# A PSUM bank for the samples' softmax, prompt attention in a lane of its own, and parted gathers

## The chip, the cores and the metric

The kernel runs on one core of a Trainium2 chip, in one launch. The metric is device time in microseconds (us). Three runs of the kernel before took 1416.22, 1419.79 and 1420.54 us; their median, 1419.79 us, is the time to compare with. What can be told from no change is about 0.3% of it, some 4.3 us.

## The reference, cut to what matters

One inference step of one layer on 512 prompt tokens and on 8 samples, each of which has 4096 past positions in a paged cache.

```python
conv_in, a, b, z, qa, kva = split_in(rmsnorm(h, g_attn) @ w_in)          # one combined projection
q, k, v, g, beta = gdn_prep(causal_conv(ext, w_conv), a, b, ...)         # group A
o_gdn = gdn_output(gdn_chunked(q, k, v, g, beta), z, g_gdn_out)          #   prompt: delta rule in chunks of 64
o_mla = mla_prompt_attention(q_nope, q_rope, k_nope, k_rope, v)          # group B, prompt: causal softmax, 8 heads
# group B, samples: for every page of the cache
kn_p, v_p = mla_expand(ckv_pool[pages], w_kv_b, g_k_nope)                #   keys are expanded to be normed
sc_p = (qn . kn_p + qr . kr_pool[pages]) * SCALE;  online softmax;  acc += p @ v_p
h = h + concat(o_gdn, o_mla) @ w_o;  h = h + ffn(rmsnorm(h));  h + (p @ w_ple_proj) * sigmoid(...)
```

Everything is float32; a weight product is made of three products of a high and a low part.

## The kernel before, in words

The spine of the program is the loop over the samples' keys at the end of `kern`: 8 samples of 32 key tiles of 128 positions. For a tile, TensorE transposes the gathered latents (`ps_cT`, L1387), ScalarE and VectorE split them (`cth`, `ctl`), and 12 matmuls of 260 columns (`ps_K`, L1453) give the expanded keys, with the sample's four scores of each half as extra columns. ScalarE squares the keys (`sqk`), VectorE sums them (`ssq`), and every 8 tiles GpSimd makes their norms (`key_norms`).

When the 32 tiles of a sample are done, `softmax_pv` works as a generator: a maximum over all keys with two small matmuls (`ps_m`), the exponential `pw`, then 33 matmuls of the weights with the gathered latents (`ps_pv`, L1358), then the sums (`ps_l`). It advances by a step per key tile of the next sample. The gathered latents of a sample stay in their buffers until `ps_pv` has read them. These buffers (`raw`, four tiles each, eight per sample) are a ring of `NR0 + NR1 = 11`; `gathers` also fetches the rotary keys (`kr`, ring of `NKR = 10`) in the same breath. `rotary` multiplies them with the rotary queries.

All else that does not depend on the samples is a filler: `mixers` is one generator through latent heads, projection (`project_qkv`, `convolve`, `gate`), then `delta_rule` and `prompt_heads` side by side (weights 0.6 and 0.4), then `split_mixers`. Per key tile it advances by `PACE = 1.45` steps. Heads of the prompt's attention therefore come only when the projection is over.

PSUM has eight banks: four for `ps_mm` (two buffers of two), one for `ps_c` (the transposed latents), one for `ps_s`, one each for `ps_f0` and `ps_f1`. `pss` hands out `ps_s`: to the softmax of the samples (`ps_m`, `ps_pv`, `ps_l`), to `rotary`, and in `prompt_heads` to the transposed keys and to the transposed probabilities `ps_pT` (L785). `psf(0)` carries one half of the projection, the convolution's transposes, the prompt's queries, scores (`ps_sc`) and output (`ps_o`, L796); `psf(1)` the other half and all of `delta_rule`. A bank that is asked for anew waits until its last reader is done.

The order in which each engine runs is fixed when the program is built: a scheduler with a timeline estimate places the instructions of the loop, which the program gives it in the order told above, and every engine then works through its own list in order. So an instruction that waits holds up all that stands behind it on its engine.

In `delta_rule`, per-row factors go to DRAM (`fac_d`, 48 rows of 512, L1013) and come back spread over partitions: `db` (L1037) for each of four tiles, 24 pieces of 64 floats for every partition, and `bk` (L1123) for the scaling on GpSimd at L1124.

After the loop come the output projection (`ps_wog`, `ps_wom`), the feed-forward and the gate, in one stretch of matmuls that the change does not touch.

Of the kernel before, what the change touches and what calls it, by code (L numbers as in the profile page):

```python
# [16 lines left out]
P = 128  # L17
# [11 lines left out]
PACE = (1.45, 1.45, 1.45)  # L29
# [40 lines left out]
def kern(tc, I, O, dbg=None, stop=99):  # L70
# [137 lines left out]
    NR0, NR1, NKR = 4, 7, 10  # L208
# [472 lines left out]
    def project_qkv(tiles):
# [3 lines left out]
        for i in tiles:  # L685
            w = load_win(i)
            ct = cv.tile([P, NT], F32, tag="ct", name=f"ct{i}")
            for hf in range(2):
                ps = psf(hf, f"ps_in{i}{hf}")
# [12 lines left out]
            conv = convolve(i, ct, psf(0, f"ps_n{i}")) if i < 12 else gate(i, ct)  # L702
# [3 lines left out]
    def gate(i, ct):  # L706
        th = cv.tile([P, NT], F32, tag="th", name=f"thz{i}")
# [36 lines left out]
    def prompt_heads():  # L744
        mh = mhp[0]
        for h in range(8):
            vv = mh.tile([P, 4, P], F32R, tag="vv", name=f"vv{h}")
            nc.sync.dma_start(f(vv), v_d[:, :, h].rearrange("p t a c -> p t (a c)"))
            parts = []
            for src, lab in ((q_d, "q"), (k_d, "k")):  # L750
                nat = mh.tile([P, 4, 96], F32, tag=lab + "n", name=f"{lab}n{h}", bufs=1)
                nc.sync.dma_start(nat, src[:, :, h, :])
                pk = psf(0, f"ps_{lab}T{h}") if lab == "q" else pss(f"ps_{lab}T{h}")
# [9 lines left out]

            off = (0, 512, 896, 1152)
            pth = mh.tile([P, 1280], F32R, tag="pth", name=f"pth{h}", bufs=1)
            ptl = mh.tile([P, 1280], F32R, tag="ptl", name=f"ptl{h}", bufs=1)
            for i in range(4):
# [208 lines left out]
    def delta_rule():  # L976
# [149 lines left out]
        for _ in range(3):  # L1126
            yield
# [558 lines left out]
```

## Time and profile before

| | us |
|---|---|
| median of three runs | 1419.79 |
| the profiled execution, its own time | 1427.76 |
| its span, first to last instruction | 1426.0 |
| TensorE matmuls busy in the span | 1349.3 (95%) |
| VectorE, ScalarE, GpSimd busy | 815.9, 586.8, 640.0 |
| mean granted clock of TensorE | 0.958 |

The loop over the keys begins near 97 us; the last key tile and the output projection lie before 945 us, and from there to the end at 1426 us there is nothing but the tail. In the profile the granted clock is 1.0 at 2.4 GHz and 0.5 at 1.2 GHz, so a stretch with 0.90 spent a fifth of its time at the lower level. The busy time of TensorE counts what runs at the lower level in full; to see what a stretch lost, one needs both its idle time and its clock.

### The profile page before, as it was taken

How to read it: one execution, taken by the hardware profiler on the slowest of the kernel's cores; microseconds unless marked ns; L12 is line 12 of the kernel's file. 1: busy time of each engine (PE TensorE's matmuls, PEld its weight loads, DVE VectorE, ACT ScalarE, POOL GpSimd, SP SyncE). 2: the span in 40 equal slices, each digit the busy share in tenths (PEclk: the TensorE clock that was granted, in tenths of full speed). 3: DMA queues.
4: the chain of work that ended last, by engine and by line, in shares of the span. 5: the costliest groups of instructions: out<-in, count | busy, mean ns of one | idle time of the engine just before them, and what ended most of it. 6: DMA issues, size and time to landing. Idle time of an engine off the chain costs nothing.

```text
span 1426.0 us, 27926 instructions
## 1 busy us (share of the span) xinstructions
PE 1349.3 (95%) x11094; PEld 1273.6 (89%) x11094; DVE 815.9 (57%) x1659; ACT 586.8 (41%) x1342; POOL 640.0 (45%) x809
## 2 busy tenths in 40 slices
PE   4889988999999898999999998999999999999998
PEld 2789977999988796997897896999999999999998
DVE  3747784655669575565683674546666566411164
ACT  3336543543455464644452464433222222222232
POOL 5222645453354497435342333546444444454531
PEclk8899998999999999999996898999999999999999
DMA  7322215234233415304323403243333333233231
GB/s 262 104 104 82 88 56 176 55 70 127 83 86 66 160 31 161 87 27 132 52 43 95 125 13 106 76 132 90 89 89 90 94 99 90 85 90 95 88 111 39
DMA packets 198806, 133.61 MB, mean 94 GB/s; under 512 B 65272, under 2 KB 183315, under 8 KB 198668
## 3 DMA queue, kind: packets, MB, share of 16 engines
q1 hardware_dynamic: 187412, 94.06, 24.2%
q0 software_dynamic: 11264, 37.76, 7.9%
q8 instruction: 88, 1.44, 0.4%
q14 instruction: 42, 0.34, 0.1%
HBM read 117.89 MB, written 14.00 MB: 92 GB/s over the span
## 4 chain that ended last, share of the span: by engine, by line
PE 80%; DVE 8%; DMA 4%; issue 4%; ACT 2%; POOL 1%; SPq 1%; another core or an unknown queue 1%; DVEq 0%; ACTq 0%; POOLq 0%
PE ps_K L1453 21%; PE ps_d L1588 9%; PE ps_u L1270 9%; PE ps_g L1270 9%; PE ps_in L693 7%; PE ps_pg L1270 3%; PE ps_cT L1387 3%; PE ps_pv L1358 2%; PE ps_wom L1549 1%; PE ps_wog L1300 1%; PE ps_natB L375 1%; DVE ssq L1458 1%; PE ps_natA L375 1%; PE ps_pp L1621 1%; PE ps_kr L1319 1%
## 5 line engine op out<-in xcount | busy, mean ns | idle before, releaser
L1453 PE MATMUL ps_K<-wkh,cth 128*128 128x260 f32 x1024 | 226.8, 301 | 10.7 <-ACT S L1457 6.4
L1458 DVE TENSOR_REDUCE ssq<-sqk 128x8 f32<-128x512 f32 x256 | 173.8, 681 | 85.6 <-ACT sqk L1456 80.5
L1456 ACT ACTIVATE sqk<-ps_K 128x512 f32<-128x512 f32 x256 | 152.7, 597 | 157.5 <-PE ps_K L1453 134.0
L1453 PE MATMUL ps_K<-wkl,cth 128*128 128x260 f32 x1024 | 215.9, 290 | 0.0
L1453 PE MATMUL ps_K<-wkh,ctl 128*128 128x260 f32 x1024 | 215.5, 291 | 0.0
L1453 PEld LDWEIGHTS ps_K<-wkh,cth 128*128 128x128 f32 x1024 | 165.0, 195 | 14.0 <-ACT S L1457 7.1
L1453 PEld LDWEIGHTS ps_K<-wkl,cth 128*128 128x128 f32 x1024 | 164.9, 195 | 0.1
L1453 PEld LDWEIGHTS ps_K<-wkh,ctl 128*128 128x128 f32 x1024 | 163.2, 194 | 0.6 <-issue 0.3
L1393 DVE TENSOR_TENSOR ctl<-ps_cT,cth 128x512 fp32r<-128x512 f32 x128 | 87.5, 684 | 48.3 <-ACT cth L1392 43.4
L1392 ACT ACTIVATE cth<-ps_cT 128x512 fp32r<-128x512 f32 x128 | 77.1, 602 | 46.0 <-PE ps_cT L1387 36.3
L336 POOL DMA_INDIRECT kr<-in_cache_krope_dram,idx x64 | 62.7, 979 | 69.2 <-PE ps_kr L1314 54.8
L334 POOL DMA_INDIRECT raw<-in_cache_ckv_dram,idx x64 | 61.4, 959 | 55.0 <-PE ps_pv L1358 26.3
L126 POOL TENSOR_TENSOR wg_l<-wg_r,wg_h 128x1024 fp32r<-128x1024 f32 x22 | 53.6, 2436 | 71.9 <-ACT wg_h L125 71.9
L1387 PE MATMUL ps_cT<-cst,raw 128*128 128x128 f32 x512 | 81.5, 282 | 3.0 <-DVE ctl L1393 2.1
L126 POOL TENSOR_TENSOR wu_l<-wu_r,wu_h 128x1024 fp32r<-128x1024 f32 x22 | 52.7, 2396 | 66.6 <-ACT wu_h L125 66.6
L126 POOL TENSOR_TENSOR wd_l<-wd_r,wd_h 128x1024 fp32r<-128x1024 f32 (+1 forms) x24 | 53.0, 2210 | 65.8 <-ACT wd_h L125 65.8
L693 PE MATMUL ps_in<-xh,win_h 128*128 128x260 f32 x256 | 73.6, 288 | 0.7 <-ACT win_h L125 0.7
L102 POOL TENSOR_SCALAR rs<-ssq 128x64 f32<-128x64 f32 x24 | 7.0, 290 | 148.6 <-DVE ssq L1458 130.4
L693 PE MATMUL ps_in<-xh,win_l 128*128 128x260 f32 x256 | 72.6, 285 | 0.0
L693 PE MATMUL ps_in<-xl,win_h 128*128 128x260 f32 x256 | 72.3, 283 | 0.0
L1270 PE MATMUL ps_g<-ul,wg_h 128*128 128x260 f32 x352 | 71.0, 283 | 0.9 <-DVE ul L1517 0.7
L1270 PE MATMUL ps_u<-uh,wu_l 128*128 128x260 f32 x352 | 71.7, 283 | 0.0
(597 smaller groups left out, 3638.4 us busy)
## 6 DMA issues: line engine op xcount, KB each, us to landing
wg_r<-in_w_ffn_gate_dram SPq DMA_DIRECT2D x22, 512.0 KB
wu_r<-in_w_ffn_up_dram SPq DMA_DIRECT2D x22, 512.0 KB
win_r<-in_w_in_dram SPq DMA_DIRECT2D x32, 256.0 KB
wd_r<-in_w_ffn_down_dram SPq DMA_DIRECT2D x16, 512.0 KB
wpg_r<-in_w_ple_gate_dram SPq DMA_DIRECT2D x8, 512.0 KB
db<-fac_d SPq DMA_DIRECT2D x8, 384.0 KB
wd_r<-in_w_ffn_down_dram SPq DMA_DIRECT2D x8, 384.0 KB
xres<-xT_d SPq DMA_DIRECT2D x8, 260.0 KB
```

Of the source, the lines that this page charges most:

```text
L126: gp.tensor_tensor(out=lo, in0=raw, in1=f(hi), op=ALU.subtract)
L334: gp.indirect_dma_start(out=raws[G].rearrange("p t c -> p (t c)"), out_offset=None, in_=ckv_rows, in_offset=off)
L336: gp.indirect_dma_start(out=krs[G], out_offset=None, in_=kr_rows, in_offset=off)
L693: te.matmul(ps[:, :HN], w[q][a][:, k, :], (xh, xl)[b][:, q * 4 + k, hf * HN:(hf + 1) * HN], start=q + k + a + b == 0, stop=q + k == 4 and ...
L1270: te.matmul(o[hf], w[a][:, k, :], mov[b][:, k, hf * HN:(hf + 1) * HN], start=k == 0 and (a, b) == (0, 0), stop=k == K - 1 and a == 1)
L1387: te.transpose(pt[:, (s * 2 + k) * P:(s * 2 + k + 1) * P], raw[:, (n % 2) * 2 + s, k * P:(k + 1) * P], ident)
L1392: sc.activation(hi, p4, AF.Copy)
L1393: ve.tensor_tensor(out=lo, in0=p4, in1=f(hi), op=ALU.subtract)
L1453: te.matmul(pk[:, hf, :260], x[:, s * 2 + k, :], y[:, k, hf, c0:c0 + 260], start=k == 0 and x is cur[0] and y is wkh, stop=k == 1 and x is ...
L1456: sc.activation(sq, pk[:, :, wo:wo + 256], AF.Square)
L1458: ve.tensor_reduce(out=ssq[:, i, :], in_=sq.rearrange("p f (h c) -> p (f h) c", h=4), axis=AX.X, op=ALU.add)
L1588: te.matmul(ps[:, hf, :HN], w[a][:, k, :], (fh, fl)[b][:, q0 + k, hf * HN:(hf + 1) * HN], start=q0 + k == 0 and a + b == 0, stop=q0 + k == ...
```

## The change

- `prompt_heads` asks `psf(0)` alone, for everything. The projection, the convolution and the gate ask `psf(1)` alone, which they share with `decays` and `delta_rule`. `ps_s` is left to the softmax of the samples and to `rotary`.
- `prompt_heads` is a lane of its own: `others` advances `mixers` and `prompts` by their own rates for each stage (`PACE`), so the heads start when the latents are done, beside the projection; a third lane, `merge`, begins `split_mixers` when both have ended. Its tiles lie beside the projection's in SBUF, so several rings get shorter: weights 3 to 2, `th`, `y`, `vv`, `pe` 2 to 1, `raw` 11 to 10, `kr` 10 to 8.
- A head is finished for each tile of 128 queries: probabilities of all key tiles are split by one ScalarE and one VectorE instruction, then multiplied with the values 128 queries at a time, in place of one product over 512 queries at the head's end.
- The rotary gathers leave `gathers` and stand in the loop, one at each pair of tiles from tile 4 on.
- The factors go to DRAM in pieces of 64 columns (`fch_d`), so that a partition of `db` reads one run of 1536 floats; `bk` is loaded in two rounds.

```diff
-PACE = (1.45, 1.45, 1.45)
+PACE = ((1.45, 0.0, 0.0), (1.2, 0.55, 0.0), (0.97, 0.55, 1.0))
-    NR0, NR1, NKR = 4, 7, 10
+    NR0, NR1, NKR = 4, 6, 8
@@ gathers
-            krs[G] = dr0.tile([P, P], F32, tag="kr", name=f"kr{G}", bufs=NKR)
             with tc.high_priority(1500):
                 gp.indirect_dma_start(out=raws[G]..., in_=ckv_rows, in_offset=off)
-                gp.indirect_dma_start(out=krs[G], out_offset=None, in_=kr_rows, in_offset=off)
+    def gather_rotary():
+        G = len(krs)
+        krs[G] = dr0.tile([P, P], F32, tag="kr", name=f"kr{G}", bufs=NKR)
+        gp.indirect_dma_start(out=krs[G], out_offset=None, in_=kr_rows, ...)
@@ project_qkv
-                ps = psf(hf, f"ps_in{i}{hf}")
+                ps = psf(1, f"ps_in{i}{hf}")
-            conv = convolve(i, ct, psf(0, f"ps_n{i}")) if i < 12 else gate(i, ct)
+            conv = convolve(i, ct, psf(1, f"ps_n{i}")) if i < 12 else gate(i, ct)
@@ prompt_heads
-                pk = psf(0, f"ps_{lab}T{h}") if lab == "q" else pss(f"ps_{lab}T{h}")
+                pk = psf(0, f"ps_{lab}T{h}")
-                pt = pss(f"ps_pT{h}{i}")
+                pt = psf(0, f"ps_pT{h}{i}")
...
+                sc.activation(pth, pt[:, :n_], AF.Copy)
+                ve.tensor_tensor(out=ptl, in0=pt[:, :n_], in1=f(pth), op=ALU.subtract)
+                yield
+                acc = psf(0, f"ps_o{h}{i}")[:, :P]
                 for j in range(i + 1):
-                    sc.activation(pth[:, o], pt[:, j * P:(j + 1) * P], AF.Copy)
-                    ve.tensor_tensor(out=ptl[:, o], in0=pt[:, j * P:(j + 1) * P], in1=f(pth)[:, o], op=ALU.subtract)
+                    for n2, b in enumerate((pth, ptl)):
+                        te.matmul(acc, vv[:, j, :], b[:, j * P:(j + 1) * P], start=j + n2 == 0, stop=j == i and n2 == 1)
+                o_ = oTm[e:e + 64, h // 2, qs]
...
-            acc = psf(0, f"ps_o{h}")
-            for j in range(4):
-                    te.matmul(acc[:, j * P:], vv[:, j, :], b[:, off[j]:off[j] + w_], ...)
@@ delta_rule
-        nc.sync.dma_start(fac_d, facT)
+        nc.sync.dma_start(fch_d.rearrange("n r c -> r n c"), facT[8:32, :].rearrange("r (n c) -> r n c", n=8))
+        nc.sync.dma_start(fac_d[32:48, :], facT[32:48, :])
-                nc.sync.dma_start(db[e * 64:(e + 1) * 64], fac_d[8:32, c0:c0 + 64].rearrange("(a h) c -> a h c", a=3)
-                                  .partition_broadcast(64))
+                nc.sync.dma_start(db[e * 64:(e + 1) * 64].rearrange("p a h c -> p (a h c)"),
+                                  fch_d[2 * t + e].rearrange("r c -> (r c)").partition_broadcast(64))
@@ the loop over the keys
-    filler = mixers() if stop != 4 else iter(())
+    lanes = [[mixers(), 0.0], [prompts(), 0.0]] if stop != 4 else []
+    def others(rates):
+        for i, l in enumerate(lanes):
+            l[1] += rates[i]
+            while l[0] is not None and l[1] >= 1.0:
+                l[1] -= 1.0
+                if next(l[0], lanes) is lanes:
+                    l[0] = None
+        if lanes and lanes[0][0] is None and lanes[1][0] is None and len(lanes) == 2:
+            lanes.append([merge(), 0.0])
+        if 4 <= i0 < 20:
+            gather_rotary()
-            pace += PACE[stage[0]]
-            while pace >= 1.0:
-                next(filler, None)
-                pace -= 1.0
+            others(PACE[stage[0]])
```

Three places of TensorE's list show what moved. The first is the softmax of sample 5 (`ps_m5`), during the key tiles of sample 6 (`ps_K6` and the tile's number; `cth`, `ctl` and `raw` carry the numbers of pairs of tiles and of gathers). `ps_og`, `ps_dS`, `ps_kS`, `ps_vn` are the chunk steps of the delta rule, `ps_pT52` the third query tile of head 5. Before:

```order
L1453 MATMUL ps_K611_10109<-wkh_99,ctl101_10015 128x260 x2
...
L785 MATMUL ps_pT52_9632<-cst_141,pe52_9582 128x128 x3
L1191 MATMUL ps_dS6_7785<-vn6_7709,k_nat_86 128x128 x4
L1164 MATMUL ps_kS7_7835<-S_6534,kq_81 64x128 x4
L1339 MATMUL ps_m5_9736<-cst_141,m85_9717 8x128
L1172 MATMUL ps_vn7_7842<-r7_7840,tts_6096 64x64 x8
L1345 MATMUL ps_m5_9736<-d85_9740,cst_141 128x8
...
L785 MATMUL ps_pT53_9744<-cst_141,pe53_9682 128x128 x4
L1191 MATMUL ps_dS7_7927<-vn7_7871,k_nat_86 128x128 x4
L796 MATMUL ps_o5_9805<-pth5_9339,vv5_9229 128x512
```

Now:

```order
L1476 MATMUL ps_K64_9958<-wkh_99,ctl98_9900 128x260 x2
L1347 MATMUL ps_m5_9880<-cst_141,m85_9851 8x128
L1199 MATMUL ps_dS1_7272<-vn1_7207,k_nat_86 128x128 x4
L1476 MATMUL ps_K65_9984<-wkh_99,cth98_9899 128x260 x2
...
L787 MATMUL ps_pT53_9591<-cst_141,pe53_9555 128x128 x4
L1353 MATMUL ps_m5_9880<-d85_9884,cst_141 128x8
L1476 MATMUL ps_K66_10038<-wkh_99,cth99_9954 128x260 x2
```

The softmax came after tile 11, behind the last chunk steps of the delta rule; now it comes at tile 4, with key tiles between, and the delta rule is at its second chunk. The second place is the end of the softmax of sample 3, during the tiles of sample 4: from the second `ps_m3` to the first tile that needs a new gather (`ps_cT` from `raw`). Before:

```order
L1345 MATMUL ps_m3_7257<-d83_7261,cst_141 128x8
L785 MATMUL ps_pT21_7265<-cst_141,pe21_7232 128x128 x2
...
L1358 MATMUL ps_pv3_7394<-raw24_4349,pw_116 32x256 x4
...
L1361 MATMUL ps_pv3_7394<-cnew_105,pw_116 32x256
L1387 MATMUL ps_cT70_7728<-cst_141,raw35_7470 128x128 x4
L785 MATMUL ps_pT22_7439<-cst_141,pe22_7366 128x128 x3
L1453 MATMUL ps_K412_7803<-wkh_99,cth70_7733 128x260 x2
```

Now:

```order
L1353 MATMUL ps_m3_7322<-d83_7326,cst_141 128x8
L797 MATMUL ps_o32_7384<-pth32_7301,vv3_6427 128x128
...
L1366 MATMUL ps_pv3_7473<-raw24_4346,pw_116 32x256 x4
...
L773 MATMUL ps_sc33_7496<-kTh3_6464,qTh3_6436 128x512
...
L1369 MATMUL ps_pv3_7473<-cnew_105,pw_116 32x256
L1395 MATMUL ps_cT68_7575<-cst_141,raw34_7565 128x128 x4
L1377 MATMUL ps_l3_7774<-cst_141,ls_117 128x1
```

The first new gather was `raw35`, for tile 12; with the shorter ring it is `raw34`, for tile 8. The third place is the projection: two halves or tiles that follow each other. Before, on two banks:

```order
L693 MATMUL ps_in61_2715<-xh_95,win61_l_2624 128x260
L1453 MATMUL ps_K117_3095<-wkh_99,cth24_2898 128x260
L693 MATMUL ps_in60_2628<-xh_95,win60_h_2617 128x260
L693 MATMUL ps_in60_2628<-xl_96,win60_h_2617 128x260
L693 MATMUL ps_in60_2628<-xh_95,win60_l_2618 128x260
```

Now, on one bank (`ps_n7` is the convolution's transpose of tile 7, and `ps_in90` the next user of the bank):

```order
L735 MATMUL ps_n7_3040<-cst_141,kq_81 128x128 x4
L1476 MATMUL ps_K126_3568<-wkh_99,cth29_3452 128x260
L1476 MATMUL ps_K126_3568<-wkl_100,cth29_3452 128x260 x2
...
L1322 MATMUL ps_kr16_3697<-cst_141,kr14_3012 128x128
...
L1476 MATMUL ps_K127_3623<-wkh_99,ctl29_3453 128x260 x2
L1395 MATMUL ps_cT31_3671<-cst_141,raw15_2562 128x128 x4
L698 MATMUL ps_in90_3242<-xh_95,win90_h_3231 128x260
```

Where the second half stood directly behind the first, there is now a key tile or more between two uses of the bank.

## Rows read from the trace of the kernel before

**Rows 1.** The page, busy time of the engines.

```profile
PE 1349.3 (95%) x11094; PEld 1273.6 (89%) x11094; DVE 815.9 (57%) x1659; ACT 586.8 (41%) x1342; POOL 640.0 (45%) x809
```

**Rows 2.** Windows: length, busy time of five engines, TensorE's clock, DMA share, GB/s.

```profile
205.00:226.00 21.00, 11.16 (x93) 7.05 (x92) 7.12 (x19) 3.33 (x7) 15.24 (x25) 0.79 0.79 267
226.00:343.00 117.00, 117.00 (x967) 116.82 (x967) 73.50 (x124) 56.72 (x128) 55.67 (x66) 0.98 0.28 68
343.00:366.00 23.00, 23.00 (x215) 19.56 (x214) 10.76 (x17) 8.74 (x21) 14.75 (x21) 1.00 0.76 238
462.00:482.00 20.00, 14.51 (x134) 9.96 (x135) 8.27 (x18) 4.85 (x10) 11.80 (x11) 0.86 0.75 249
...
545.00:575.00 30.00, 24.81 (x232) 18.98 (x233) 13.03 (x34) 12.61 (x36) 19.40 (x40) 0.89 0.73 193
...
645.00:678.00 33.00, 31.37 (x264) 25.05 (x264) 16.87 (x46) 15.42 (x41) 18.52 (x51) 0.90 0.38 130
...
752.00:796.00 44.00, 42.26 (x265) 32.08 (x262) 13.28 (x34) 10.41 (x25) 11.77 (x25) 0.61 0.39 126
...
856.00:897.00 41.00, 33.12 (x249) 27.65 (x247) 18.43 (x45) 22.06 (x57) 17.36 (x28) 0.83 0.33 104
...
945.00:1426.00 481.00, 474.37 (x3951) 470.91 (x3950) 225.89 (x262) 138.53 (x191) 208.52 (x97) 1.00 0.30 89
```

**Rows 3.** Timeline of PE, softmax of sample 6: start, length, operation [idle <-releaser].

```profile
861.11 0.27 PE L1339 MATMUL ps_m<-cst,m 128*8 128x128 f32 x1 [1.73 <-DVE ptl L789]
862.08 0.51 PE L1345 MATMUL ps_m<-d,cst 8*128 8x8 f32 x2 [0.70 <-DVE d L1343]
863.62 6.30 PE L1358 MATMUL ps_pv<-raw,pw 128*32 128x256 f32 x64 [1.04 <-ACT pw L1348]
...
872.71 0.90 PE L785 MATMUL ps_pT<-cst,pe 128*128 128x128 f32 x3 [1.66 <-ACT asb L1366]
```

**Rows 4.** Timeline of PE, end of the softmax of sample 5.

```profile
751.24 0.40 PE L1453 MATMUL ps_K<-wkh,ctl 128*128 128x260 f32 x2
...
772.57 4.45 PE L1358 MATMUL ps_pv<-raw,pw 128*32 128x256 f32 x38
...
789.52 0.80 PE L1453 MATMUL ps_K<-wkh,cth 128*128 128x260 f32 x2
```

**Rows 5.** Timeline of PE, softmax of sample 3 and the gather behind it.

```profile
549.10 6.54 PE L1358 MATMUL ps_pv<-raw,pw 128*32 128x256 f32 x64 [0.97 <-DVE ptl L789]
...
556.88 0.66 PE L1387 MATMUL ps_cT<-cst,raw 128*128 128x128 f32 x4 [0.69 <-DMA raw<-in_cache_ckv_dram,idx]
...
558.22 0.51 PE L1453 MATMUL ps_K<-wkh,cth 128*128 128x260 f32 x2 [0.32 <-ACT cth L1392]
```

**Rows 6.** Timeline of POOL, the gather that row 556.88 waited for.

```profile
551.01 1.00 POOL L334 DMA_INDIRECT raw<-in_cache_ckv_dram,idx  x1 [0.16 <-issue]
```

**Rows 7.** Timeline of SP's queue, the factors' first loads.

```profile
415.93 9.20 SPq L1037 DMA_DIRECT2D db<-fac_d  x4
```

**Rows 8.** Timeline of DVE, where the factors are first read.

```profile
426.47 0.69 DVE L1040 TENSOR_TENSOR dd<-db,gcl 128x512 f32<-128x512 f32 x1 [6.11 <-issue]
427.08 0.25 DVE L1321 COPY srp<-ps_kr 128x96 f32<-128x96 f32 x1
```

**Rows 9.** Timeline of PE at the same place.

```profile
427.38 0.44 PE L785 MATMUL ps_pT<-cst,pe 128*128 128x128 f32 x2 [2.81 <-DVE srp L1321]
```

**Rows 10.** Timeline of PE, matmuls of 128 queries at the end of head 6.

```profile
886.03 0.22 PE L796 MATMUL ps_o<-pth,vv 128*128 128x128 f32 x1
886.09 0.62 PE L1387 MATMUL ps_cT<-cst,raw 128*128 128x128 f32 x4
...
886.69 0.31 PE L796 MATMUL ps_o<-ptl,vv 128*128 128x128 f32 x1
886.83 0.46 PE L1453 MATMUL ps_K<-wkh,cth 128*128 128x260 f32 x2
```

**Rows 11.** Source line L697, the projection's way out of its bank: min/median/max ns.

```profile
L697 DVE TENSOR_TENSOR ct<-ps_in,rb x32: 416/428/430, 236.1 to 391.9; 128x260 f32<-128x260 f32 x32
```

More of the change, by code (lines that the diff above doesn't have):

```diff
@@ L706, in gate @@
     def gate(i, ct):
[L707 removed]
+        th = cv.tile([P, NT], F32, tag="th", name=f"thz{i}", bufs=1)
         sc.activation(th, ct, AF.Tanh, scale=0.5)
@@ L762, in prompt_heads @@
             Q, K = parts
-            off = (0, 512, 896, 1152)
-            pth = mh.tile([P, 1280], F32R, tag="pth", name=f"pth{h}", bufs=1)
-            ptl = mh.tile([P, 1280], F32R, tag="ptl", name=f"ptl{h}", bufs=1)
+            e = (h % 2) * 64
             for i in range(4):
@@ L807, in kern @@
     fac_d = dram.tile([48, SEQ], F32, name="fac_d")
+    fch_d = dram.tile([8, 24, 64], F32, name="fch_d")
     A_d = dram.tile([2, 64, 32, 32], F32, name="A_d")
@@ L1116, in delta_rule, with load_bk @@
                 nc.sync.dma_start(xt[r0_, t], X6[n2, :, t])
-        for j in range(4):
-            bk = gb.tile([P, 2, SEQ], F32, tag="bk", name=f"bk{j}")
+        def load_bk(j):
+            bk = gb.tile([P, 2, SEQ], F32, tag="bk", name=f"bk{j}", bufs=2)
             for a in range(2):
@@ L1123, in delta_rule @@
                     nc.sync.dma_start(bk[e * 64:(e + 1) * 64, a, :], fac_d[r_].partition_broadcast(64))
-            gp.tensor_tensor(out=kq[:, :, j, :SEQ], in0=kq[:, :, j, :SEQ], in1=bk, op=ALU.mult)
-        for _ in range(3):
-            yield
+            return bk
+        bks = [load_bk(0), load_bk(1)]
+        yield
+        yield
+        for j in range(4):
+            gp.tensor_tensor(out=kq[:, :, j, :SEQ], in0=kq[:, :, j, :SEQ], in1=bks[j], op=ALU.mult)
+            if j < 2:
+                bks.append(load_bk(j + 2))
+                yield
+        yield
         for t2 in range(2):
@@ L1403, in mixers, with project_and_delta, prompts, merge @@
         cv = px.enter_context(pool("cv", 2, side="right"))
-        yield from decays()
+        pmh = ExitStack()
+        mhp.extend((pmh.enter_context(pool("mh", 2)), pmh))
         stage[0] = 1
-        yield from project_qkv((4, 5, 6, 7, 8, 9, 10, 11, 12, 13, 14, 15, 0, 1, 2, 3))
-        px.close()
-        pmh = ExitStack()
-        mhp.append(pmh.enter_context(pool("mh", 2, side="right")))
-        stage[0] = 2
-        two = [[delta_rule(), 0.6, 0.0], [prompt_heads(), 0.4, 0.0]]
-        while two:
-            for g in list(two):
-                g[2] += g[1]
-                while g[2] >= 1.0:
-                    g[2] -= 1.0
-                    if next(g[0], two) is two:
-                        two.remove(g)
-                        break
+        def project_and_delta():
+            yield from decays()
+            yield from project_qkv((4, 5, 6, 7, 8, 9, 10, 11, 12, 13, 14, 15, 0, 1, 2, 3))
+            px.close()
+            stage[0] = 2
+            yield from delta_rule()
+        yield from project_and_delta()
+    def prompts():
+        while not mhp:
             yield
-        pmh.close()
+        yield from prompt_heads()
+    def merge():
+        mhp[1].close()
         mid.close()
         yield from split_mixers()
-    filler = mixers() if stop != 4 else iter(())
+    lanes = [[mixers(), 0.0], [prompts(), 0.0]] if stop != 4 else []
[8 more added lines that the diff above has]
+            lanes.append([merge(), 0.0])
     soft = iter(())
-    pace = 0.0
     cur = None
@@ L1475, in kern @@
             soft = softmax_pv(b, S_, srp)
-    for _ in filler:
-        pass
+    while any(l[0] is not None for l in lanes):
+        others((1.0, 1.0, 1.0))
     for _ in project_delta():
```

31 lines of the change are left out of this document (13 added, 18 removed).

## The prediction

> **What bounds the kernel now.** I read the page's busy times first, then windows of TensorE's idle time and granted clock, then its timeline with releasers, and last the queue and engine that each releaser names. The page has TensorE busy for 1349.3 of 1426 us, and no other engine above 57% [rows 1]; so the time is TensorE's own work plus what it loses, idle or at the lower clock. A window shows both: its length less TensorE's busy time is idle, and (1 − clock) times its length is what the lower level took, since the clock column is 1.0 at 2.4 GHz and 0.5 at 1.2 GHz. The tail, 945 to 1426, runs at 1.00 and is not touched, and the projection, 226 to 343, is full [rows 2]. The loss that the change can reach lies in seven short stretches, one for each sample's softmax while the next sample's keys are made. Idle + clock, from [rows 2]: sample 0 9.8 + 4.4 = 14.2; sample 1 0 + 0, under the projection; sample 2 5.5 + 2.8 = 8.3; sample 3 5.2 + 3.3 = 8.5; sample 4 1.6 + 3.3 = 4.9; sample 5 1.7 + 17.2 = 18.9; sample 6 7.9 + 7.0 = 14.9. That is 69.7 us in all, and 55.5 for samples 2 to 6.
>
> **What makes a stretch lose.** Three kinds of wait. The softmax and the heads' transposed probabilities share `ps_s`: `ps_m` waited 1.73 us for VectorE's `ptl`, the second `ps_m` 0.70, `ps_pv` 1.04 for the exponential, and `ps_pT` 1.66 for ScalarE's `asb`, which frees the softmax's bank [rows 3]; `ps_pv` of sample 3 waited 0.97 for `ptl` too [rows 5]. Then the ring of `raw`: the gather was issued at 551.01 [rows 6], when the weighted sum had read its first four tiles, and the transposes that need it began at 556.88 [rows 5], 5.9 us later. Last, the pipeline from there has to be filled: the next `ps_K` waited 0.32 for `cth` [rows 5]. Round these waits the clock falls, so `ps_pv` took 6.54 us at half speed [rows 5].
>
> **Part 1: the softmax's own bank, heads spread over the loop, ring of 10.** For samples 2 to 6:
> - The waits on `ptl` and `asb` at the bank go. What is late next is the softmax's own chain, the exponential before `ps_pv`; [rows 3] bound it by 1.04 us. In the new order key tiles and heads stand between its steps in most samples, so I take 2 us for all five.
> - The gather stays. From release to first transpose it is 5.9 + 0.3 = 6.2 us (the 0.3 is my estimate for the issue, from the 0.16 of [rows 6]). It runs beside 29 of the 33 weighted-sum matmul groups (their full-clock length is half of 6.54, 3.3, so 2.9 us), and beside 0.5 to 2.0 us of heads that the new order puts there. That leaves 1.4 to 2.8 us by sample, 10.6 for five. The ring of 10 ends the stock at tile 8 rather than tile 12; this moves the wait and does not lengthen it as long as the gather goes out at the same step of `ps_pv`.
> - Filling: 5 × 0.32 = 1.6.
> - The clock: one fall of the size in samples 2 to 4 (2.8 to 3.3) for each of these again, and half of that, 1.7, for samples 5 and 6, where no end of the delta rule and no block of finishing heads stands in the stretch: 3 × 3.3 + 2 × 1.7 = 13.3.
>
> Sum 2 + 10.6 + 1.6 + 13.3 = 27.5 against 55.5: **−28**. The nearest rows for the bounds: if each stretch is as good as sample 4 (4.9), 24.5 and −31; if none falls in clock, 14.2 and −41; as bad as sample 6 (14.9) each, 74.5 and +19.
>
> **Part 2: the factors as one run.** VectorE stood 6.11 us at `dd` until `db` had come, `srp` stood behind it [rows 8], and TensorE waited 2.81 us for `srp` [rows 9]; the four loads took 9.20 us of the queue [rows 7]. Pieces of 256 B become runs of 6 KB. What is queued behind `dd` is now no head's bank, since `rotary` alone shares `ps_s`. Between 0 and −2.8; I take **−2**. The Trainium skill (DMA: Bandwidth & Descriptors, Specifications) asks for at least 512 B in a transfer for full rate. By it the loads gain, but the new store `fch_d`, 192 pieces of 256 B where 48 rows of 2 KB went, loses; as the loads had 1536 such pieces each, my estimate by it is under 1 us, and no row here shows the store as late.
>
> **Part 3: a head finished for each 128 queries.** The product with the values was 8 matmuls a head over 512, 384, 256 and 128 queries, 2560 columns; it is 20 of 128, the same 2560. For eight heads 64 become 160. Only the spacing of short ones can cost: [rows 10] have two neighbours that start 0.06 us (886.03 to 886.09) and 0.14 us (886.69 to 886.83) after a 128-query matmul. Against 0.06, which is the columns alone, 160 cost 0 to 160 × 0.08 = 12.8; below nothing is excluded, as the columns are equal. I take 0.09, near the lower row, as the 0.14 stands at a change of the moving tile's kind: 160 × 0.03 = **+5**. The Trainium skill (TensorE: Matmul & The Clock Gate, Back-to-back issue gap) gives about 81 ns for sustained pairs of weight load and matmul with 128 columns, against an isolated formula of about 56; by it this part would be an estimated 160 × 0.021 = +3.4, and the 0.06 of the row says that such a matmul need not pay it. Splitting the probabilities in 2 instructions for a tile of queries, not 2 for each 128 by 128, takes work off ScalarE and VectorE, which are 41% and 57% busy [rows 1]: nothing.
>
> **Part 4: the projection on one bank.** Two banks took turns; now every half, convolution and gate waits until its forerunner has left `psf(1)`: 16 tiles × 3 = 48 hand-overs. The way out is one VectorE instruction of 0.428 us [rows 11] or longer chains at the convolution. If TensorE stood at each, 48 × 0.43 = 20.6. In the new order about 12 key matmuls stand between most uses of the bank; a pair of them takes 0.40 us [rows 4], so 12 take some 2.4 us in the profile's lengths, some five times the evacuation. Between 0 and +20.6, I take seven stalls, **+3**. Below nothing has no reason: this window is full now.
>
> **Part 5: sample 0.** Its stretch comes before the heads, with a bank that nobody shared; only the shorter ring reaches it. 0 to +4 (its own clock loss, 4.4, a second time); I take **+1**. The rotary gathers, parted from `raw`'s, unblock GpSimd, and `bk` in two rounds uses half the buffer: GpSimd is busy 45% of the span [rows 1] and is waited for only through `raw`, which part 1 has. Nothing; if this cover fails, it is rival A. Shorter weight rings: hidden by the DMA share of 0.28 in the projection [rows 2].
>
> **Sum.** −28 − 2 + 5 + 3 + 1 = **−21**. The profiled execution took 1427.76, so 1406.8; it stands 8.0 above the median of the runs, 1419.79, and on that footing the forecast is **1399 us**.
>
> **Rivals.**
> - **A, slower: the stock of keys ends too early.** With a ring of 10 the softmax must be through by tile 8, and the delta rule's chain and two new lanes share the same steps, so every stretch of samples 2 to 6 costs what sample 6's cost, 14.9 [rows 2]. Then part 1 is 74.5 − 55.5 = +19, and with the other parts' +7 the time is 1420 + 26 = 1446. It decides from (55.5 − 7)/5 = 9.7 us a stretch upward; the present mean is 11.1. For it: TensorE already waits for gathers, and the new order gives 4 tiles less of stock. Against: 11.1 is made by samples 5 and 6, whose waits are named as the shared bank. Chance 0.19.
> - **B: the fall of clock in sample 5 belongs to the delta rule.** Between 752 and 796 TensorE is idle for only 1.7 us, but at 0.61 [rows 2], and among its last chunk steps no key tile runs from 751.24 to 789.52 [rows 4]. If those small matmuls, not the waits, hold the clock down, they keep doing it elsewhere, and 17.2 − 1.7 = 15.5 of the gain is not there: −5.5, 1414 us. Against: they run between key tiles after the change, and samples 3 and 4 have delta steps with 3.3 [rows 2]. Chance 0.20, half of it within 0.3%.
> - **C: the clock stays up in all five.** With the heads as cover the 13.3 go as well, −34, 1385 us. For it: the projection's cover leaves sample 1 at 1.00 and no idle [rows 2]. Against: the gather still outlasts its cover. Chance 0.18.
>
> **How the numbers follow.** The forecast has 0.43. Its own range is 1388 to 1412: down by part 3 (5), part 4 (3), part 5 (1) and the exponential's 2 us at nothing, up by part 3 at 0.14 (8), part 2 at nothing (2) and part 4 twice as large (3). Leaving out the far half of C and of A, about 0.2, the range is 1380 to 1432. A measurement can tell 0.3%, 4.3 us. Faster by more: the forecast (0.43, less 0.02 for its upper end), C (0.18) and half of B (0.10): 0.69. Within 0.3%: the other half of B and 0.02: 0.12. Slower: A, 0.19.
>
> **What would show it.** Windows over the seven stretches: idle about 14 and clock loss about 13 in samples 2 to 6 together; over 70 is A, one stretch at 0.6 beside delta steps is B, clock of 0.97 and more throughout is C. In the timeline `ps_m` no longer waits for `ptl`, nor `ps_pT` for `asb`; the transposes of tile 8 wait for `raw` by 1.4 to 2.8 us a sample. VectorE's wait before `dd` shrinks below 3 us, and nothing on TensorE waits for `srp`. Neighbouring 128-query `ps_o` matmuls start 0.09 us apart; 0.14 would be +13. TensorE waits for `ct` and the convolution by some 3 us in all; over 10 would make the forecast wrong, as would an end of the loop that comes later with the stretches clean, which would mean the heads' lane ends after the keys.

## The result, and the profile after

The changed kernel took 1403.18 us, the median of five runs (1398.23 to 1407.83), against 1419.79 (1416.22 to 1421.03) for the kernel before beside it: ratio 0.9879, 95% interval 0.9854 to 0.9905, or 16.6 us less. The forecast was 1399, or 21 less. Two later sets with the same pair gave 0.9858 (0.9827 to 0.9889) and 0.9869 (0.9827 to 0.9912). The profiled execution took 1398.23 us, the shortest of the five; that of before, 1427.76, was longer than all five runs of before. So the traces differ by 29.5 us, and some 13 of it is where the two executions fell, not the change.

The page's busy times, after [rows 1]:

```profile
PE 1334.1 (96%) x11190; PEld 1266.1 (91%) x11190; DVE 817.7 (59%) x1635; ACT 585.3 (42%) x1318; POOL 639.5 (46%) x809
```

Windows after [rows 2], columns as there: sample 0, the stretch with the projection, then samples 2, 3, 4, 5 and 6, the end of the loop, the tail:

```profile
195.00:222.00 27.00, 15.15 (x121) 11.44 (x122) 10.02 (x26) 3.17 (x7) 18.52 (x28) 0.75 0.71 232
222.00:442.00 220.00, 220.00 (x1872) 215.79 (x1871) 143.49 (x295) 120.60 (x301) 92.36 (x133) 1.00 0.27 72
442.00:465.00 23.00, 20.05 (x165) 16.77 (x163) 14.36 (x45) 7.47 (x19) 12.82 (x16) 0.85 0.50 163
533.00:555.00 22.00, 19.45 (x161) 15.21 (x160) 10.63 (x27) 8.75 (x23) 16.65 (x35) 0.84 0.61 202
618.00:640.00 22.00, 19.60 (x207) 16.61 (x206) 5.87 (x12) 7.19 (x16) 10.29 (x17) 0.84 0.84 246
718.00:737.00 19.00, 19.00 (x148) 16.09 (x147) 9.73 (x21) 8.67 (x23) 12.35 (x36) 0.91 0.59 192
805.00:830.00 25.00, 25.00 (x229) 19.55 (x228) 12.99 (x30) 8.48 (x24) 8.89 (x17) 1.00 0.42 139
830.00:917.00 87.00, 82.57 (x715) 78.62 (x715) 51.32 (x109) 42.79 (x103) 39.85 (x69) 1.00 0.39 113
917.00:1396.00 479.00, 472.46 (x3936) 468.97 (x3934) 227.09 (x261) 138.53 (x191) 208.46 (x96) 1.00 0.30 89
```

Idle plus (1 − clock) times length: samples 2 to 6 lose 6.4, 6.1, 5.9, 1.7 and 0, together 20.1 us where it was 55.5. Sample 0 loses 18.6 (was 14.2). The projection and all to 442 us are full at clock 1.00. The row of the loop's end, 830 to 917, has 4.4 us of idle time that the sum did not have; the same stretch of before has 0.4:

```profile
897.00:945.00 48.00, 47.58 (x428) 45.01 (x427) 24.74 (x57) 16.60 (x39) 22.88 (x29) 1.00 0.37 111
```

TensorE in the softmax of sample 2, which has the waits that are left [rows 3, 5]:

```profile
447.60 0.38 PE L1353 MATMUL ps_m<-d,cst 8*128 8x8 f32 x2
449.54 3.66 PE L1366 MATMUL ps_pv<-raw,pw 128*32 128x256 f32 x64 [1.12 <-ACT pw L1356]
...
455.72 0.66 PE L1395 MATMUL ps_cT<-cst,raw 128*128 128x128 f32 x4 [0.94 <-DMA raw<-in_cache_ckv_dram,idx]
457.25 0.38 PE L1377 MATMUL ps_l<-cst,ls 128*128 128x1 f32 x2 [0.88 <-ACT asb L1374]
```

No step of the softmax waits for a head's `ptl` any more. In sample 6 no step waits at all; key tiles stand between the parts of the weighted sum:

```profile
811.55 0.38 PE L1353 MATMUL ps_m<-d,cst 8*128 8x8 f32 x2
...
816.90 1.93 PE L1366 MATMUL ps_pv<-raw,pw 128*32 128x256 f32 x30
...
821.52 1.48 PE L1366 MATMUL ps_pv<-raw,pw 128*32 128x256 f32 x18
```

### The profile page after: what moved, and what is told of

The parts are those of the page before. It is cut to its first block, busy times and chain, and to the rows that moved or that the text cites. A ratio compares the mean times of both kernels' runs of the same rounds, so it can differ in the third digit from the quotient of the medians.

```text
span 1396.1 us, 28086 instructions
## 1 busy us (share of the span) xinstructions
PE 1334.1 (96%) x11190; PEld 1266.1 (91%) x11190; DVE 817.7 (59%) x1635; ACT 585.3 (42%) x1318; POOL 639.5 (46%) x809
## 3 DMA queue, kind: packets, MB, share of 16 engines
q1 hardware_dynamic: 175808, 94.05, 24.6%
## 4 chain that ended last, share of the span: by engine, by line
PE 81%; DVE 7%; DMA 5%; issue 3%; SPq 1%; POOL 1%; ACT 1%; another core or an unknown queue 0%; DVEq 0%; POOLq 0%; ACTq 0%
PE ps_K L1476 21%; PE ps_d L1608 9%; PE ps_u L1278 9%; PE ps_g L1278 9%; PE ps_in L698 7%; PE ps_cT L1395 4%; PE ps_pg L1278 3%; PE ps_pv L1366 2%; PE ps_wom L1569 1%; PE ps_wog L1308 1%; PE ps_natB L380 1%; DVE ssq L1481 1%; PE ps_o L797 1%; PE ps_pp L1641 1%; DMA db<-fch_d 1%
## 5 line engine op out<-in xcount | busy, mean ns | idle before, releaser
L1476 PEld LDWEIGHTS ps_K<-wkh,cth 128*128 128x128 f32 x1024 | 161.1, 193 | 6.1 <-issue 3.9
L127 POOL TENSOR_TENSOR win_l<-win_r,win_h 128x512 fp32r<-128x512 f32 x32 | 41.1, 1290 | 70.4 <-ACT win_h L126 69.4
```

The source lines that it names most:

```text
L127: gp.tensor_tensor(out=lo, in0=raw, in1=f(hi), op=ALU.subtract)
L1476: te.matmul(pk[:, hf, :260], x[:, s * 2 + k, :], y[:, k, hf, c0:c0 + 260], start=k == 0 and x is cur[0] and y is wkh, stop=k == 1 and x is ...
```

## The experiments

One measure for all traces. A softmax stretch here runs from 6 us before `ps_m` to 3 us behind the last `ps_l`, and its loss is TensorE's idle time plus half the time at 1.2 GHz; the bounds are a little wider than the windows above, so by this measure the kernel before lost 56.2 in samples 2 to 6. "End" is the same loss from the last key matmul to the first `ps_g`, the feed-forward's first product; the output projection lies between (in before it ends at 969 us, not by 945). "wog" is when the output projection (`ps_wog`) starts, counted from the last key matmul. All in us; every kernel was timed against the kernel before on its own chip.

| kernel | ratio to before (95%) | first key | sample 0 | samples 2 to 6 | wog | end |
|---|---|---|---|---|---|---|
| before | 1 | 92.3 | 15.1 | 56.2 | −21.7 | 0.4 |
| before, again | 0.9997 (0.9969 to 1.0025) | 92.2 | 15.2 | 57.7 | −21.7 | 0.4 |
| changed | 0.9879 (0.9854 to 0.9905) | 87.7 | 20.5 | 20.4 | −11.7 | 1.1 |
| changed, again | 0.9858 (0.9827 to 0.9889) | 88.6 | 19.7 | 20.7 | −11.7 | 1.1 |
| changed, beside the queries on VectorE | 0.9869 (0.9827 to 0.9912) | 89.3 | 22.1 | 10.8 | −13.3 | 0.8 |
| bank alone | 1.0135 (1.0109 to 1.0160) | 92.0 | 15.3 | 16.2 | +60.1 | 66.7 |
| bank shared | 1.0166 (1.0139 to 1.0192) | 90.8 | 21.5 | 60.2 | −29.0 | 1.8 |
| ring of 11 | 0.9933 (0.9907 to 0.9958) | 89.4 | 14.8 | 24.6 | +10.5 | 17.9 |
| rotary gathers back | 0.9980 (0.9959 to 1.0000) | 91.4 | 21.2 | 22.4 | −1.8 | 11.7 |
| ring of 11, heads first | 1.0008 (0.9993 to 1.0022) | 90.6 | 17.7 | 26.3 | +20.1 | 29.4 |
| lanes first | 0.9935 (0.9914 to 0.9955) | 89.3 | 10.2 | 24.8 | −1.8 | 10.2 |
| before, gathers parted | 1.0019 (0.9995 to 1.0042) | 92.7 | 6.4 | 39.2 | −21.6 | 0.4 |
| queries on VectorE | 0.9962 (0.9943 to 0.9980) | 89.6 | 18.1 | 9.1 | +0.1 | 13.1 |
| queries on VectorE, again | 0.9929 (0.9902 to 0.9956) | 92.5 | 18.1 | 9.6 | +0.3 | 11.7 |

**Before, again.** No edit.

> The kernel before, unchanged, for a second trace. If the profiled 1427.76 us was one execution that lay high, the median is 1416 to 1421 again, and this trace's span is nearer to 1418; then the first key matmul, at 92.3 us before and 87.7 us after the change, moves by some us without any change, and this part of the difference between the two traces is no effect. Samples 2 to 6 should lose 45 to 60 us of idle and clock together again. Rival: the 4.6 us at the start belong to the change, and first keys stand at 92 us again.

Median 1426.98, and this chip's runs of before 1426.49. The profiled execution took 1430.45, 3.5 above the median, so a long profiled execution was not a single case. The losses come again almost to the number, in sample 5 too (0.61 of full clock, 17.1 us). The first key matmul stayed at 92.2.

**Bank alone.** The kernel before with two lines:

```diff
-                pk = psf(0, f"ps_{lab}T{h}") if lab == "q" else pss(f"ps_{lab}T{h}")
+                pk = psf(0, f"ps_{lab}T{h}")
-                pt = pss(f"ps_pT{h}{i}")
+                pt = psf(0, f"ps_pT{h}{i}")
```

> The kernel before, and only the heads' transposes moved off the softmax's bank, to the bank of the scores (ring of 11, heads after the projection as before). Theory A, the bank makes the loss of the softmax stretches: samples 2 to 6 lose at most 25 us together where they lost 55.5; but a head on one bank is a chain with one query tile at a time, and by the order one head and a half are left when the keys have run out, so from the last key matmul to the first ps_g it takes some 75 us instead of 49. Sum -30 + 26: 1410 to 1422 us. Theory B, the heads spread beside the projection hide the softmax, the bank hardly matters: samples 2 to 6 lose 45 to 60 again, and with the bare end the time is 1435 to 1450.

Theory A is right on the stretches (16.2 for 56.2), and wrong on the end: from the last key matmul to the first `ps_g` it took 114.5 us where it had taken 49, 65 more and not 26, and 66.7 of it is loss. So the kernel is slower than before by 1.35%, where the theory had 1410 to 1422 us. Windows of samples 3 and 5, and of the end:

```profile
524.00:547.00 23.00, 21.52 (x204) 18.66 (x203) 13.74 (x32) 10.24 (x28) 19.47 (x34) 1.00 0.41 125
...
698.00:731.00 33.00, 32.20 (x303) 26.84 (x302) 21.46 (x50) 13.57 (x41) 17.27 (x22) 1.00 0.70 163
...
870.00:985.00 115.00, 77.33 (x555) 65.74 (x555) 41.58 (x104) 38.55 (x79) 40.81 (x27) 0.75 0.27 79
```

The keys are done at 870 us, 50 earlier than before; the last head then stands alone, each step waiting for the one before it:

```profile
910.78 0.90 PE L785 MATMUL ps_pT<-cst,pe 128*128 128x128 f32 x3 [2.73 <-ACT pe L782]
913.64 0.80 PE L771 MATMUL ps_sc<-kTh,qTh 96*128 96x512 f32 x1 [1.96 <-DVE ptl L789]
918.36 1.11 PE L785 MATMUL ps_pT<-cst,pe 128*128 128x128 f32 x4 [3.07 <-ACT pe L782]
```

What I had not counted is that the output projection comes behind it (930 us), with its weights' waits and at the lower clock.

**Bank shared.** The changed kernel with these two lines put back (`ps_kT` and `ps_pT` on `ps_s`).

> The changed kernel, with the heads' key transposes and transposed probabilities back on the softmax's bank; lane, ring of 10, single projection bank and all else stay. Theory A: all softmaxes slip to the end of the stock of keys (tile 8, with no key tile between their steps), samples 2 to 6 lose 50 to 75 us where the changed kernel loses 20, time 1430 to 1455 us, no faster than before. Theory B: they lose 20 to 30 and the time is 1403 to 1412.

As theory A has it: 60.2 in the stretches, 1449.29 us. With lane, parting and spread all there, the stretches' loss of before is back. Windows of samples 2 and 6, and TensorE in sample 6:

```profile
455.00:496.00 41.00, 32.37 (x236) 24.46 (x235) 22.35 (x60) 12.30 (x33) 18.73 (x29) 0.79 0.56 164
...
860.00:900.00 40.00, 30.04 (x214) 24.27 (x213) 21.37 (x46) 13.96 (x37) 15.76 (x27) 0.79 0.33 109
```

```profile
877.34 5.82 PE L1366 MATMUL ps_pv<-raw,pw 128*32 128x256 f32 x64
...
887.89 0.55 PE L787 MATMUL ps_pT<-cst,pe 128*128 128x128 f32 x3 [3.60 <-ACT asb L1374]
```

**Ring of 11.** The changed kernel with `NR0, NR1, NKR = 4, 7, 7`, `asb` in the buffer of `krT`, and

```diff
-        if 4 <= i0 < 20:
+        if 4 <= i0 < 18 or i0 == 26:
```

> The changed kernel with a ring of 11 for the latents, as before; the 4 KB come from one rotary buffer less (its eighth gather moves to tile 26) and from one buffer shared by krT and asb. Theory: in sample 0 TensorE waits 5.7 us for the maximum because 4 key tiles of stock less stand in front of it, 4 x 12 matmuls of 0.12 us = 5.8; with them back, sample 0 loses 13 to 15 us where the changed kernel loses 18.6, and the wait for a gather after ps_pv goes in samples 3 to 6: 1393 to 1399 us. Rival: weights and queries from DRAM end that stretch, and what is saved at the maximum is waited for at ps_qT or ps_in; then 1401 to 1406, as the changed kernel.

Sample 0 does what was expected: 14.8, and the wait of 5.7 us for the maximum is gone. In the changed kernel it was:

```profile
198.88 0.38 PE L1347 MATMUL ps_m<-cst,m 128*8 128x128 f32 x1 [5.70 <-DVE m L1344]
```

The waits for gathers did not go as expected: one of 2.64 us is left in sample 3, and samples 2 to 6 lose 24.6. The time does not follow: 0.9933, worse than the changed kernel's 0.9858 on the same chip. The rival's reason does not hold either. The loss is at the end, 17.9 us: keys ran ahead, the last head ended behind them, and `ps_wog` starts 10.5 us after the last key.

**Rotary gathers back.** The changed kernel, `gather_rotary()` called in `gathers` again, `NKR` 10.

> The changed kernel, with each rotary gather issued behind its latent gather again (ten buffers for them, as before); all else stays. The prediction priced the parting at nothing: ratio to the changed kernel 0.998 to 1.002. Rival, the gathers of the start: with ten rotary gathers in GpSimd's queue and on the DMA engines before the first keys, the first key matmul stands at 91 to 92 us, not 88 to 90, and the time is 3 to 5 us longer than the changed kernel's.

Neither: 1420.02 against 1399.31 for the changed kernel beside it, 20.7 us more. The two traces are 25.7 us apart: the first key matmul comes 2.8 later, first to last key take 12.1 more, and from there to the first `ps_g` it is 11.2 more. The softmax stretches have only 2 of it (22.4 for 20.7). So with the gathers back nothing of the change's gain is left (0.9980), although the bank is free and the heads have their lane.

**Before, gathers parted.** The same edit by itself, the other way round: TensorE's order is that of before.

> The kernel before, and only the rotary gathers parted from the latent ones and put into the loop (ring of 10 kept); the order of TensorE's instructions is that of before. The run with the gathers put back lost some 17 us against the changed kernel. Theory C, the gathers themselves: less in GpSimd's queue and on the DMA engines at the start (first key matmul at 88 to 89.5 us instead of 92) and no blocked queue later: 6 to 17 us under before. Theory D, the start alone: 2 to 5 us under before, and the rest of the 17 us comes from the other order that the scheduler made of that kernel: softmax stretches of samples 2 to 6 as before, 50 to 60 us.

1404.84 against 1403.60: nothing, and the first key stood at 92.7. In this order theory C falls, and D's start with it. For the run above that leaves another order of the instructions as the likely reason, which is not shown: the queries on VectorE (below) have nearly its order (96% of the two lists of TensorE stand in the same sequence), with the gathers parted, and cost 8.3 of the 20.7 us, on another chip; the other 12 stay open. TensorE waited little longer for the latent gathers there (3.5 us in all, 1.5 in the changed kernel). The losses of this trace are smaller than those of before (39.2 for 56.2); its chip, where before, too, took 1403.6, may be the reason, but there is no trace of before from it.

**Ring of 11, heads first.**

```diff
+        while True:
+            with tc.high_priority(600):
+                if next(heads, heads) is heads:
+                    return
+            yield
```

> The kernel of the ring of 11, with the instructions of the prompt's heads preferred by the scheduler (600 places ahead in its order). Theory: the ring did what it should (sample 0 at 14.7), and the 71 us from the last key matmul to the first ps_g, against 52 in the changed kernel, came from heads that fell behind the keys. With the heads done before the last key tile, this part takes at most 60 us, sample 0 loses 14 to 16, samples 2 to 6 at most 26: 5 to 12 us under the changed kernel. Rival: TensorE's work only changes places, the last key tile comes later by what the end saves: within 4 us of the ring of 11 alone, 3 to 9 us above the changed kernel.

The last head ended at 841 us, 49 before the last key, and yet the end lost 29.4: `ps_m` of the last sample waited 18.27 us for VectorE.

```profile
908.97 0.38 PE L1347 MATMUL ps_m<-cst,m 128*8 128x128 f32 x1 [18.27 <-DVE m L1344]
```

(What VectorE did in that time is shown under the last heading.) Before it, VectorE still had the delta rule's last gating to do, which in this order came behind the last key:

```profile
896.73 0.69 DVE L1255 TENSOR_TENSOR kq<-kq,zs 128x520 f32<-128x520 f32 x1
```

The heads first, the delta rule ended last. At 1423.66 us, 24 above the changed kernel, both the theory and its rival fail: an early end of the heads is not enough.

**Lanes first.** The changed kernel, the same context with 300 round each step of every lane.

> The changed kernel (ring of 10), with the instructions of all lanes beside the samples preferred by the scheduler (300 places). By the order sample 0's softmax then stands alone (no projection matmuls in it) and the last head ends at tile 20 of sample 7. Theory: it is the bank and an end of the heads before the last key tile that count, and both are there already, so the preference gives nothing: within 4 us of the changed kernel. Rival: the keys lose their cover as in the bank shared kernel, 10 us and more above it.

1413.33, 14 us above the changed kernel: the theory fails. It is the rival's size, but not its reason, since samples 2 to 6 lose only 4 more (and sample 0 loses 9.5 less, which does not show in the time: first to last key take 804 us for 800). The end has 10.2: `ps_wog` started 1.8 us before the last key.

**Queries on VectorE, twice, and the changed kernel as control.** One word: `gp.tensor_tensor` to `ve.tensor_tensor` in the scaling of the prompt's queries.

> The changed kernel, with the prompt queries' scaling (eight instructions) on VectorE instead of GpSimd. Local theory: in sample 0 VectorE's two-operand instructions took 1.07 to 1.21 us instead of 0.28 beside these GpSimd instructions, so the maximum, 5.7 us late, comes 2 to 3 us sooner, and ps_qT's wait of 4.3 us for the queries from DRAM shrinks by as much. But the order of the whole program changes with it: from sample 2 on it is nearly that of the kernel with the gathers put back, with the output projection's first matmuls behind the last key tile. Theory D (order): then it is 8 to 17 us slower than the changed kernel although its gathers are parted. Theory C (gathers): 0 to 4 us faster than the changed kernel.

> The changed kernel, unchanged, for a second trace beside the others of this set. Ratio to the kernel before again 0.985 to 0.991. If the start belongs to the change, the first key matmul stands near 88 us again (92.0 to 92.3 in all three traces of the old order of gathers); if it was one execution, at 89 to 91. Samples 2 to 6 lose 15 to 26 us together, sample 0 loses 17 to 20.

> The changed kernel, unchanged, as control for the run beside it. On the chip of the last pair the kernel before took 1403.6 us, where it took 1419.8 to 1426.5 on the others, so what the change gives may depend on the chip. If the changed kernel takes about 1400 us wherever it runs, its ratio is 0.985 to 0.990 on a chip where before takes 1420 and above, and 0.995 to 1.000 where before takes 1404.

> The changed kernel with the queries' scaling on VectorE, beside the changed kernel on one chip. Its trace lost 9.1 us in samples 2 to 6 and 13.1 us between the last key matmul and the first ps_g; the changed kernel's 20.7 and 1.1. Local theory: 0 to 6 us faster than the changed kernel beside it. Theory D (the other order costs): 8 to 17 us slower.

Beside each other on one chip: 1396.47 and 1388.21, so the edit costs 8.3 us, the lower end of theory D; across chips the first run could not be read. The keys ended 10.5 us sooner, but from there to the first `ps_g` it took 13.9 us longer. The local part came in half: `ps_qT` waits 2.33 us for the queries instead of 4.95, but the maximum is 5.63 late as before (5.69). The guess that the changed kernel takes 1400 us everywhere falls: its ratio stays, 0.986 to 0.988, whether before takes 1406 or 1422. Windows from the last key to `ps_g`, first with the queries on VectorE, then the changed kernel:

```profile
871.00:937.00 66.00, 58.69 (x497) 54.67 (x497) 32.33 (x57) 18.63 (x30) 35.11 (x23) 0.93 0.38 113
```

```profile
882.00:933.00 51.00, 50.24 (x468) 47.36 (x467) 31.39 (x56) 16.41 (x25) 26.51 (x19) 1.00 0.42 125
```

And what TensorE waits for in the first of them:

```profile
876.48 0.51 PE L1308 MATMUL ps_wog<-ah,wog_l 128*128 128x260 f32 x2 [3.75 <-POOL wog_l L127]
883.84 0.38 PE L1347 MATMUL ps_m<-cst,m 128*8 128x128 f32 x1 [3.17 <-DVE m L1344]
```

Over all kernels of the table the loss at the end goes with the start of `ps_wog`: at most 1.8 us where it starts 11 us or more before the last key, 10 to 13 where it starts with it, 18 to 67 where it starts after. Then the split of its weights on GpSimd and the last sample's softmax have nothing beside them. On GpSimd one can read what comes before that start. In the changed kernel three weights are split (`wog_l`) ahead of the low parts of the mixers (`al`); in the queries on VectorE, in rotary gathers back and in lanes first all eight `al`, 10 us, stand in front. The changed kernel, then the queries on VectorE:

```profile
873.40 2.54 POOL L127 TENSOR_TENSOR wog_l<-wog_r,wog_h 128x512 fp32r<-128x512 f32 x2
...
877.55 3.81 POOL L1296 TENSOR_TENSOR al<-kq,ah 128x520 fp32r<-128x520 f32 x3
```

```profile
870.25 4.96 POOL L1296 TENSOR_TENSOR al<-oTm,ah 128x512 fp32r<-128x512 f32 x4
875.17 3.74 POOL L127 TENSOR_TENSOR wog_l<-wog_r,wog_h 128x512 fp32r<-128x512 f32 x3
```

Before had that order too, but its heads ended 33 us before the last key. All this is a relation over ten kernels, not an edit of that start alone; none was tried.

## Why the prediction was right

The direction and the size held, and in the softmax stretches the mechanism too: with the bank given they lose 16 to 20 us, with the bank taken back 60. The time has a second condition that the prediction had put at nothing: the order at the loop's end. Five edits that leave bank and lane as they are (ring of 11, heads first on top of it, rotary gathers back, lanes first, queries on VectorE) cost 8 to 24 us. That the order made for the changed kernel had `ps_wog` start 11.7 us before the last key was luck, as far as the prediction goes. By its own steps:

- **Part 1, −28: measured −35.** Idle 7.9 us (forecast 14) and clock 12.2 (forecast 13.3). The step that was mis-sized is the wait for the gather: 10.6 in the sum, in the trace about 1 us in samples 2 and 3 and none behind them, where key tiles and heads stand between the parts of the weighted sum. (Its 3.3 us for the weighted sum at full clock, half of 6.54, misreads [rows 5]: the last tenth of those 6.54 us ran at 2.4 GHz, as the window's clock of 0.55 says, and at 1.00 the same matmuls now take 3.66.)

```profile
549.10:555.64 6.54, 6.54 (x65) 2.95 (x66) 1.16 (x4) 1.50 (x3) 5.46 (x6) 0.55 0.74 214
```

  The prediction had the softmax come before tile 8 for the shorter ring; in the order of bank alone it begins at tiles 4 to 8 with a ring of 11, so it is the bank that lets it come early.
- **Part 2, −2: measured −2.4, and −0.9 in two other traces; wrong in reason.** The loads are no faster. VectorE's first `dd` began 10.5 us after the first load's issue before (415.93 to 426.47, [rows 7, 8]) and 10.1 after:

```profile
463.95 19.30 SPq L1037 DMA_DIRECT2D db<-fch_d  x6
...
474.04 0.69 DVE L1040 TENSOR_TENSOR dd<-db,gcl 128x512 f32<-128x512 f32 x1 [2.11 <-DMA db<-fch_d]
...
476.38 0.66 PE L1395 MATMUL ps_cT<-cst,raw 128*128 128x128 f32 x4 [0.40 <-DVE ctl L1401]
```

  What stands behind `dd` is now `ctl`, and TensorE waits 0.40 us for it here (1.90 in the second and third traces), where it waited 2.81 [rows 9]. VectorE's wait before `dd` was to shrink below 3 us; it was 2.11, and 3.59 and 3.62 in the other two.
- **Part 3, +5: right.** From each `ps_o` matmul's start to the next instruction's, idle time and half of the time at the lower clock taken off, the 64 took 12.7 us and the 160 take 17.9: +5.1. In the whole trace the second of a row of them starts 0.06 us after the first, as in [rows 10], and each further one 0.11 after the one before; the sum had 0.09:

```profile
551.70 0.22 PE L797 MATMUL ps_o<-pth,vv 128*128 128x128 f32 x1
551.76 0.28 PE L797 MATMUL ps_o<-ptl,vv 128*128 128x128 f32 x1
551.87 0.28 PE L797 MATMUL ps_o<-pth,vv 128*128 128x128 f32 x1
551.99 0.27 PE L797 MATMUL ps_o<-ptl,vv 128*128 128x128 f32 x1
```

- **Part 4, +3: nothing.** The window 222 to 442 has no idle time.
- **Part 5, +1: +4.4.** The ring's price was put too low: ring of 11 takes 5 to 6 us of it back, as 4 key tiles less stood before the maximum.
- **The end, not in the sum: some +4** (4.4 us of idle time for 0.4). `ps_wog` waits for `al` in the changed kernel:

```profile
876.01 0.40 PE L1308 MATMUL ps_wog<-ah,wog_h 128*128 128x260 f32 x2
878.88 0.50 PE L1308 MATMUL ps_wog<-al,wog_h 128*128 128x260 f32 x2 [2.47 <-POOL al L1296]
```

- **Parted gathers, nothing: right in the order of before, wrong in the new one.** In before that edit alone gave nothing; in the changed kernel, taking it back costs 20.7 us, nearly the whole gain of that set (22.9). The prediction looked at how busy GpSimd is and at what waits for it, not at the order that the scheduler makes with the edit; how much of the 20.7 is order stays open. The earlier first key (87.7 for 92.3) I can't give to the change: one and the same kernel had it at 89.6 and at 92.5.

Together −35.4 − 2.4 + 5.1 + 0 + 4.4 + 4 = −24.3. The two traces differ by 29.9 us, or 25.3 without the start, so the parts account for most of it; the losses outside the stretches were not split up. The medians differ by 16.6 to 23, so the forecast of 21 is nearer than its parts deserve: part 1 was too cautious by some 7, and part 5 and the end too cheap by the same.

Rival A fell (20 us in the stretches, not 74). Rival B fell: with the bank alone, sample 5 has its delta steps beside key tiles at clock 1.00 (in the window 698 to 731, one of them here); the half clock of [rows 4] goes with the stretch that had no key tiles (the run of before with parted gathers, of the same order, has it again, 14.0 us). Rival C was near for samples 5 and 6 only.

```profile
703.66 1.14 PE L1172 MATMUL ps_vn<-r,tts 64*64 64x64 f32 x16
```

None of the rivals was what decided the experiments: with the bank alone the last head ended 38 us later than before (last `ps_o` at 924.3 instead of 886.7) while the keys were done 50 us sooner, so the heads have to start earlier, which the lane lets them do. The bank without the rest, and the rest without the bank, each cost about what they gain together (1.0135 and 1.0166 against 0.9879). The single projection bank and the head finished in tiles were never tried alone.

## What to carry to other kernels

When two parts share a PSUM bank, one engine's late reader stalls the other part; giving one of them the bank frees it, but the other, on one bank less, ends later and has to start earlier: price its end, not only the waits that go. After any change of order read the stretch between the last instruction of the main loop and the tail: here seven of the runs lost 10 us or more in that stretch, far from the place that was edited. Compare kernels only with runs of the same chip beside them.

## What the runs showed of the hardware that was not expected

- **VectorE held by GpSimd.** In the run with heads first, VectorE's steps on 128x64, with two operands in SBUF, took 1.19 to 1.26 us beside GpSimd's subtractions, and 0.22 after them. VectorE, then GpSimd:

```profile
898.27 1.26 DVE L108 SCALAR_TENSOR_TENSOR rs<-rs,rs 128x64 f32<-128x64 f32 x1
899.57 1.21 DVE L109 TENSOR_TENSOR rs<-rs,rs 128x64 f32<-128x64 f32 x1
900.81 1.19 DVE L110 SCALAR_TENSOR_TENSOR rs<-rs,rs 128x64 f32<-128x64 f32 x1
...
907.18 0.22 DVE L110 SCALAR_TENSOR_TENSOR rs<-rs,rs 128x64 f32<-128x64 f32 x1
```

```profile
898.17 2.53 POOL L1296 TENSOR_TENSOR al<-kq,ah 128x520 fp32r<-128x520 f32 x2 [1.92 <-ACT ah L1295]
900.66 4.92 POOL L1296 TENSOR_TENSOR al<-oTm,ah 128x512 fp32r<-128x512 f32 x4
```

  Each VectorE step is as long as one GpSimd instruction (4.92 / 4 = 1.23). The Trainium skill (SBUF — State Buffer, SBUF: two separate sides) says that the two share a port pair as an exclusive lock, which a VectorE operation with two SBUF inputs needs; these rows agree. Seven such steps, 1 us longer each than the 0.22 after them, are some 7 of the 18.27 us that `ps_m` waited.
- **At half the clock key matmuls are not twice as slow.** Pairs of them, 260 columns each, start 0.24 us apart at 2.4 GHz and 0.44 at 1.2, 1.8 times:

```profile
446.31 0.40 PE L1476 MATMUL ps_K<-wkh,cth 128*128 128x260 f32 x2
446.55 0.40 PE L1476 MATMUL ps_K<-wkl,cth 128*128 128x260 f32 x2
...
461.20 0.64 PE L1476 MATMUL ps_K<-wkl,cth 128*128 128x260 f32 x2
461.64 0.64 PE L1476 MATMUL ps_K<-wkh,cth 128*128 128x260 f32 x2
```

  The weighted sum does take twice as long: 38 of its matmuls 4.45 us, nearly all at 1.2 GHz [rows 4], 0.117 each, and 64 of them 3.66 us at 2.4 GHz, 0.057 each. So half of a stretch's time at the lower clock overstates a little what it costs where key matmuls fill it.
- **Chips differ.** The kernel before took 1403.6, 1406.2, 1419.8, 1422.2 and 1426.5 us in five sets, the first two on two other chips than the last two; the last two, on one chip, still differ by 4.3.
